# A decoder trunk on one core: the first FFN product by Strassen's seven products of halves, in a fixed order of slots, and the FFN in two parts

## The chip, the core and the metric

The kernel runs on one core of a Trainium2 chip. A core has TensorE (PE in the profile; PEld is its loading of weights), VectorE (DVE), ScalarE (ACT), GpSimd (POOL), and SyncE (SP), whose queue issues most DMA transfers. Each engine works through its own list of instructions in order; semaphores hold an instruction until what it needs is there. PE multiplies a stationary 128x128 tile of weights with a moving tile of up to 512 columns and adds into a bank of PSUM (128 partitions x 512 fp32; there are eight). The metric is the time of one execution on the device in microseconds.

## What is computed

Two decoder layers on one sequence of 512 tokens with 1024 channels. Each has a mixer (layer 0: gated short convolution and pooling; layer 1: attention and a convolution module) and a feed-forward part (FFN), each followed by a residual and a LayerNorm:

```python
D_FF = int(math.ceil((8 * D_MODEL / 3) / 256) * 256)      # 2816
ALPHA = (2.0 * DEPTH) ** 0.25
...
def swiglu(x, w_in, w_out):
    h = x @ w_in
    return (jax.nn.silu(h[..., :D_FF]) * h[..., D_FF:]) @ w_out
...
        x = layer_norm(ALPHA * x + mix, ln_mix_g[layer], ln_mix_b[layer])
        x = layer_norm(ALPHA * x + swiglu(x, ffn_w_in[layer], ffn_w_out[layer]),
                       ln_ffn_g[layer], ln_ffn_b[layer])
```

All is fp32 in and out. The change concerns `swiglu` alone.

## The kernel before

**Exact products.** Each fp32 operand is split into a high half (a copy rounded to fp32r, on ACT: `split`, L84) and a low half (the operand less its high half, on DVE or POOL, L85). A product of two operands is three matmuls: high x high, high x low, low x high (`mm3`, L88 to L90). In the up projection the weights are stationary and the input, kept transposed and split in `xh` and `xl` (128 partitions x 8 x 512), moves.

**The FFN** (`ffn`, L293). It runs over 22 slices n of 128 hidden columns. For each, `load_cols` brings two weight tiles (128x1024, gate and up, 512 KB each) into one of three `raw` buffers and splits them into two of the eight `wt` buffers; `project` then does 2 x 8 x 3 = 48 matmuls of 512 columns into two PSUM banks (slices 0 and 1 in two halves of 256 columns, `SPLIT`). The word pair in this text means such a slice with its gate and up columns. Then silu on ACT (L316), the product on DVE (L318) and a split into `hh` and `hl`, which are kept for all 22 slices. At slice 6 (`XN`) `late_affine` applies the preceding LayerNorm's gain and offset to the residual `xs` on DVE (L202).

**The output projection** (`OutProj`). `first` goes through 11 steps of two slices for the left 512 output columns, with four banks for the four token tiles; `second` does the right 512 columns, the last 5 steps with resident weights token by token, so that `residual` and `norm` of one token tile lie beside the matmuls of the next. `residual` multiplies by ALPHA, adds and takes statistics.

**The order.** A scheduler sets the order of instructions on each engine from priorities, in the attention part PE's list is written out by hand (`tc.manual_schedule`). Buffers of a pool are given out in turn: a tile of a tag with n buffers waits until the tile n places before it is no longer used.

Of the kernel before, what the change touches and what calls it, by code (L numbers as in the profile page):

```python
# [17 lines left out]
P = 128  # L18
S = 512
# [20 lines left out]
SPLIT = [(0, 256), (256, 512)]  # L40
FIRST = 2
DFIRST = 2
DG = 1
XA = 2
XN = 6
XG = (3, 8)
# [12 lines left out]
def trunk(ctx, tc, x, ev_w_in, ev_conv_w, ev_pool_w, ev_pool_scale, ev_w_out, od_w_in,  # L59
# [108 lines left out]

    def load_gb(gb, g, b):
        nc.sync.dma_start(gb[:, 0, :], g.partition_broadcast(P))  # L170
        nc.sync.dma_start(gb[:, 1, :], b.partition_broadcast(P))
        return gb
# [18 lines left out]

    def late_affine(g, b, eng):

        gb = [wtp.tile([P, D], F32, tag="wt", name="gb") for _ in range(2)]
        for dst, v in zip(gb, (g, b)):
            nc.sync.dma_start(dst, v.partition_broadcast(P))
        with tc.high_priority(offset=-CP):
            for t in range(NT):
                for c in range(2):
                    cs = slice(c * 512, (c + 1) * 512)  # L200
                    for v, op in zip(gb, (ALU.mult, ALU.add)):
                        eng.tensor_tensor(xs[t][:, cs], xs[t][:, cs], v[:, cs], op=op)  # L202

    def norm(t, st, gb, ln):
# [11 lines left out]
        for a, b in PIECES:  # L216
            xc, g, b_ = xs[t][:, a:b], gb[:, 0, a:b], gb[:, 1, a:b]
# [12 lines left out]
    class OutProj:  # L230

        def __init__(self, w, order, lhs, resident, resident_pool=lambda kp: None, eng=None):
            self.w, self.order, self.lhs, self.resident = w, order, lhs, resident
            self.resident_pool, self.eng = resident_pool, eng
# [27 lines left out]
        def second(self, gb, ln):  # L264
            KP, order = len(self.order), self.order
            for t in range(NT):
                residual(t, slice(0, 512), self.accs[t][0][0], self.sts[t][:, 0, :])
                self.accs[t] = None
# [4 lines left out]
            for i in range(streamed):  # L273
                ws = self.load(order[i], 512)
                for t in range(NT):
                    self.step(t, i, ws)
            ws = [self.load(kp, 512, self.resident_pool(kp)) for kp in order[streamed:]]
            for t in range(NT):
                for part in range(len(self.accs[t])):
                    acc, cols = self.accs[t][part]  # L280
                    for i in range(streamed, KP):
                        self.step(t, i, ws[i - streamed], part)
                    residual(t, slice(512 + cols.start, 512 + cols.stop), acc, self.sts[t][:, 1 + part, :])
                norm(t, self.sts[t][:, :1 + len(self.accs[t]), :], gb, ln)
# [6 lines left out]


    def ffn(l):  # L293
        w_in, w_out = ffn_w_in[l], ffn_w_out[l]
        with tc.tile_pool(name=f"ffn{l}", bufs=1) as hp:
            pairs = []
            gb = hp.tile([P, 2, D], F32, tag="gb", name="gb") if l else None
            for n in range(NF):
                if n == XN:
                    late_affine(ln_mix_g[l], ln_mix_b[l], nc.vector)  # L300
                if n == 4 and l:
                    load_gb(gb, ln_ffn_g[l], ln_ffn_b[l])
                if n < FIRST and n % FIRST == 0:
# [7 lines left out]
                if n % 2 == 0:  # L311
                    tag = "hA" if n < 10 else "hB"
                    pairs.append([hp.tile([P, 2, S], F32R, tag=tag, name=nm, bufs=10 if n < 10 else 12)
                                  for nm in ("hh", "hl")])
                sg = wk.tile([P, S], F32, tag="sg", name="sg")
# [3 lines left out]
                split(pairs[-1][0][:, n % 2, :], pairs[-1][1][:, n % 2, :], h)  # L319
            out_proj(gb, 1 + 2 * l, w_out, list(range(NF // 2)), lambda k: [y[:, k % 2, :] for y in pairs[k // 2]],  # L320
                     5, lambda kp: [dict(pool_=hp, tag="hA", bufs=10)] * 2)

# [540 lines left out]
```

## Time and profile before

| | |
|---|---|
| runs | 1101.07 us median of 3 (1101.02 to 1101.72) |
| profiled execution | 1100.73 us, its span 1099.0 us |
| granted TensorE clock | 0.994 |
| busy: PE, PEld, DVE, ACT, POOL | 1077.5, 909.8, 529.7, 395.4, 179.9 us |
| FFN of layer 0 | about 165 to 524 us; of layer 1, about 742 us to the end |

In the profile a line like L85 is a line of the kernel before; a helper's line stands for all that call it. Rows of groups show the line, engine, operation, output and input by the program's names, and the shapes; then busy time, mean duration in ns, and the idle time before them with what ended it. In a timeline the columns are start and duration in us. The rows of windows give the busy time of each engine (with its count of instructions), the granted clock, the share of the DMA engines and GB/s.

### The profile page before, as it was taken

Reading aid. Unit: us, or ns where it says so; the run is one execution under the profiler, and the core shown is the slowest. Engines: PE = TensorE matmul, PEld = TensorE weight load, DVE = VectorE, ACT = ScalarE, POOL = GpSimd, SP = SyncE. Lnnn points to the kernel's source line nnn. Section 1 sums busy time; section 2 is a strip of 40 time slices with the busy share of each in tenths; the row PEclk is TensorE's granted clock in tenths of the full one; section 3 lists DMA queues with packets and bytes.
Section 4 is the critical chain, followed back from the end, with each engine's and each line's share of the span. In section 5 each row is a group of like instructions: output and inputs, shape, how many; then the busy total and the mean of one; then the engine's idle time right before and its main releaser. Section 6 shows DMA issues by size and latency. Waiting matters only on the chain.

```text
span 1099.0 us, 13519 instructions
## 1 busy us (share of the span) xinstructions
PE 1077.5 (98%) x5371; PEld 909.8 (83%) x5371; DVE 529.7 (48%) x821; ACT 395.4 (36%) x613; POOL 179.9 (16%) x163
## 2 busy tenths in 40 slices
PE   7999999999999999999999999999999999999997
PEld 7888898888888888888978777898888888888886
DVE  4845464643333332426489978464643333332426
ACT  4333243222223221223476889443222222221210
POOL 2000300000000000012499972700000000000003
PEclk9999999999999999999999999999999999999999
DMA  6423503343333222350333331413343333322312
GB/s 205 120 92 115 153 1 113 98 134 96 96 96 96 96 96 96 115 154 21 78 83 92 98 99 57 134 58 113 99 134 96 96 96 96 96 96 96 115 39 77
DMA packets 150332, 108.30 MB, mean 99 GB/s; under 512 B 5256, under 2 KB 131768, under 8 KB 150270
## 3 DMA queue, kind: packets, MB, share of 16 engines
q1 hardware_dynamic: 149648, 107.11, 32.4%
q8 instruction: 42, 0.69, 0.3%
q10 hardware_dynamic: 622, 0.34, 0.1%
q14 instruction: 20, 0.16, 0.0%
HBM read 103.17 MB, written 2.10 MB: 96 GB/s over the span
## 4 chain that ended last, share of the span: by engine, by line
PE 93%; DVE 2%; ACT 2%; DMA 1%; POOL 1%; issue 1%; SPq 0%; POOLq 0%
PE fl L88 12%; PE fl L90 12%; PE fl L89 12%; PE sc L88 9%; PE sc L90 9%; PE sc L89 9%; PE py L88 4%; PE py L89 4%; PE py L90 4%; PE cv L89 4%; PE cv L90 4%; PE cv L88 4%; PE tp L132 1%; DMA x<-in_x 1%; DVE cv L466 1%
## 5 line engine op out<-in xcount | busy, mean ns | idle before, releaser
L84 ACT ACTIVATE w<-raw 128x1024 fp32r<-128x1024 f32 x176 | 186.0, 1060 | 538.6 <-PE sc L89 176.7
L85 DVE TENSOR_TENSOR w<-raw,w 128x1024 fp32r<-128x1024 f32 x148 | 180.7, 1224 | 288.1 <-ACT w L84 287.9
L85 POOL TENSOR_TENSOR w<-raw,w 128x1024 fp32r<-128x1024 f32 x28 | 67.4, 2416 | 429.1 <-ACT w L84 415.5
L89 PE MATMUL sc<-xl,w 128*128 128x512 f32 (+1 forms) x360 | 129.9, 361 | 0.0
L90 PE MATMUL sc<-xh,w 128*128 128x512 f32 (+1 forms) x360 | 129.6, 361 | 0.0
L88 PE MATMUL sc<-xh,w 128*128 128x512 f32 (+1 forms) x360 | 129.4, 362 | 0.0
L88 PE MATMUL fl<-xh,w 128*128 128x512 f32 (+1 forms) x352 | 128.6, 366 | 0.0
L89 PE MATMUL fl<-xl,w 128*128 128x512 f32 (+1 forms) x352 | 128.4, 365 | 0.0
L90 PE MATMUL fl<-xh,w 128*128 128x512 f32 (+1 forms) x352 | 128.3, 365 | 0.0
L166 POOL TENSOR_TENSOR rs<-rs,neghalf 128x1 f32<-128x1 f32 x20 | 14.4, 720 | 413.6 <-DVE rs L165 413.6
L90 PEld LDWEIGHTS sc<-xh,w 128*128 128x128 f32 x360 | 68.0, 189 | 10.3
L89 PEld LDWEIGHTS sc<-xl,w 128*128 128x128 f32 x360 | 68.0, 189 | 10.3
L88 PEld LDWEIGHTS sc<-xh,w 128*128 128x128 f32 x360 | 67.6, 189 | 10.3
L89 PEld LDWEIGHTS fl<-xl,w 128*128 128x128 f32 x352 | 66.5, 189 | 10.5
L88 PEld LDWEIGHTS fl<-xh,w 128*128 128x128 f32 x352 | 66.4, 189 | 10.6
L90 PEld LDWEIGHTS fl<-xh,w 128*128 128x128 f32 x352 | 66.3, 189 | 10.6
L89 PE MATMUL fl<-w,hh 128*128 128x512 f32 (+1 forms) x176 | 66.3, 377 | 0.0
L88 PE MATMUL fl<-w,hh 128*128 128x512 f32 (+1 forms) x176 | 66.1, 376 | 0.0
L90 PE MATMUL fl<-w,hl 128*128 128x512 f32 (+1 forms) x176 | 66.1, 376 | 0.0
L466 DVE SCALAR_TENSOR_TENSOR cv<-hp,par,cv 128x512 f32<-128x512 f32 x84 | 63.1, 751 | 5.8 <-ACT cv L454 4.5
L89 PE MATMUL py<-xl,w 128*128 128x512 f32 (+1 forms) x160 | 58.9, 368 | 0.0
L88 PE MATMUL py<-xh,w 128*128 128x512 f32 (+1 forms) x160 | 58.9, 368 | 0.0
(364 smaller groups left out, 2050.4 us busy)
## 6 DMA issues: line engine op xcount, KB each, us to landing
raw<-in_ffn_w_in SPq DMA_DIRECT2D x88, 512.0 KB
raw<-in_ffn_w_out SPq DMA_DIRECT2D x44, 512.0 KB
raw<-in_od_w_in SPq DMA_DIRECT2D x20, 512.0 KB
raw<-in_ev_w_in SPq DMA_DIRECT2D x16, 512.0 KB
raw<-in_ev_w_out SPq DMA_DIRECT2D x8, 512.0 KB
raw<-in_od_w_out SPq DMA_DIRECT2D x8, 512.0 KB
x<-in_x SPq DMA_DIRECT2D x4, 512.0 KB
qk<-qk SPq DMA_DIRECT2D x16, 128.0 KB
```

What stands on the lines that cost most here:

```text
L84: nc.scalar.activation(hi, src, AF.Copy)
L85: (eng or nc.vector).tensor_tensor(lo, src, f32(hi), op=ALU.subtract)
L88: nc.tensor.matmul(acc, lh, rh, start=start, stop=False)
L89: nc.tensor.matmul(acc, lh, rl, start=False, stop=False)
L90: nc.tensor.matmul(acc, ll, rh, start=False, stop=stop)
L132: nc.tensor.transpose(tp[:, j * P:(j + 1) * P], xs[t][:, k * P:(k + 1) * P], ident)
L166: nc.gpsimd.tensor_tensor(rs[:, 1:2], rs[:, 0:1], neghalf, op=ALU.pow)
L466: V.scalar_tensor_tensor(acc if i == KCONV - 1 else part, hp[:, i:i + S], tap(i), part, op0=ALU.mult, op1=ALU.add)
```

## The change

Slices 0 to 3 (`PLAIN`) are projected as before. The other 18 are taken two at a time, nine groups a layer. A group's 256 gate and 256 up columns and the 1024 input channels make a 2x2 matrix of blocks of weights (512 channels x 256 columns, the tiles `q11`, `q21`, `q22`, `q12`, of 128x4x256, 512 KB each), and the input is a 2x2 matrix of blocks too (512 channels x 256 tokens). Instead of eight products of blocks the group has seven (Strassen's, in Winograd's form):

- The input's combinations are made once per layer (`moving`, 10 sums on DVE and four splits); one of them overwrites a block of `xh` and `xl`, after the plain slices have used it.
- Of the weights, four sums S1 to S4 per group (DVE, L369), and seven operands are split: high halves on ACT (`hi`, L376), low halves on DVE (`lo`, L380), in three pairs of buffers `sw`.
- Each product is 2 x 4 x 3 = 24 matmuls of 256 columns (L388). Products add up in PSUM banks x (`fl`), y (`sc`) and z (`py` or `cv`); partial sums are kept by three copies on ACT (c1, u2, u3: L396) and joined by DVE (`gate`, L403; u3, L438 and L486). `silu` and `times` act on halves of 256 tokens, `final` splits the result into `hh` and `hl`.

PE's slots in a group are P1, P4 of the last group, P2, P3 of the last group, P6, P5, P7. The order on PE, ACT and DVE is the one of the code (`manual_schedule`); after the last group of a part `closing` does its P4 and P3. The FFN has two parts: slices 0 to 11 with the output projection of these (`OutProj.first` in the fixed order, six steps, the affine steps of `xs` between them; `second` for the right columns, added to `xs` with ALPHA and without statistics), then slices 12 to 21 and their output projection, added with factor 1.

DVE's list in layer 0 before, in the steady part (L85 makes a weight's or a result's low half, L318 the gated result; the numbers are buffers):

```order
L318 TENSOR_TENSOR h_2022<-cv_1957,sg_2020 128x512
L85 TENSOR_TENSOR w_2105<-raw_2102,w_2104 128x1024
L85 TENSOR_TENSOR hl_2019<-h_2022,hh_2018 128x512
L85 TENSOR_TENSOR w_2169<-raw_2166,w_2168 128x1024
L318 TENSOR_TENSOR h_2090<-fl_2027,sg_2088 128x512
L85 TENSOR_TENSOR w_2175<-raw_2172,w_2174 128x1024
```

DVE's list now at the turn from one group to the next (`sw` halves from L380; `sum` S4 and the next S1; L410 `times`; L417 the final low half):

```order
L380 TENSOR_TENSOR sw_2042<-sum_2015,sw_2041 128x1024
L369 TENSOR_TENSOR sum_2047<-sum_1947,q12_1746 128x1024
L369 TENSOR_TENSOR sum_2080<-q21_1917,q22_1919 128x1024
L380 TENSOR_TENSOR sw_2078<-q11_1915,sw_2077 128x1024
L410 SCALAR_TENSOR_TENSOR g_1784<-u3_1906,g_1784 128x2x256
L380 TENSOR_TENSOR sw_2110<-q22_1744,sw_2109 128x1024
L417 TENSOR_TENSOR hl_1694<-g_1784,hh_1693 128x1024
L438 TENSOR_TENSOR u3_2139<-u3_2139,sc_2049 128x512
L380 TENSOR_TENSOR sw_2142<-q12_1921,sw_2141 128x1024
L369 TENSOR_TENSOR sum_2180<-sum_2080,q11_1915 128x1024
```

A slice had four operations; now the next group's P1, the last group's result, P4 and P2 stand in one sequence, in which each waits for those ahead of it. ACT at the same place, before and now (L84, L86 and L376 high halves; L316 and L406 silu; L396 copies; L415 the final high half):

```order
L84 ACTIVATE w_2726<-raw_2724 128x1024
L84 ACTIVATE hh_2570<-h_2642 128x512
L84 ACTIVATE w_2788<-raw_2786 128x1024
L316 ACTIVATE sg_2710<-fl_2646 128x512
L84 ACTIVATE w_2794<-raw_2792 128x1024
L84 ACTIVATE hh_2708<-h_2712 128x512
```

Now ACT makes all of this at the turn of a group:

```order
L376 ACTIVATE sw_2041<-sum_2015 128x1024
L406 ACTIVATE g_2012<-g_2012 128x2x256
L396 ACTIVATE u2_2074<-fl_1881 128x512
L406 ACTIVATE g_1784<-g_1784 128x2x256
L376 ACTIVATE sw_2077<-q11_1915 128x1024
L415 ACTIVATE hh_1693<-g_1784 128x1024
L376 ACTIVATE sw_2109<-q22_1744 128x1024
L396 ACTIVATE u3_2139<-fl_1881 128x512
L376 ACTIVATE sw_2141<-q12_1921 128x1024
```

ACT's copies u2 and u3 and both silu now stand among the high halves that PE needs next. The end of the up projection, ACT, before and now (now: the end of part 1):

```order
L84 ACTIVATE hh_2846<-h_2850 128x512
L84 ACTIVATE w_2992<-raw_2990 128x1024
L316 ACTIVATE sg_2916<-fl_2854 128x512
L84 ACTIVATE w_3022<-raw_3020 128x1024
L84 ACTIVATE hh_2846<-h_2918 128x512
L84 ACTIVATE w_3052<-raw_3050 128x1024
```

ACT now, from the last group of part 1 into the output projection:

```order
L415 ACTIVATE hh_1913<-g_2245 128x1024
L376 ACTIVATE sw_2559<-q22_2152 128x1024
L396 ACTIVATE u3_2564<-fl_2347 128x512
L376 ACTIVATE sw_2566<-sum_2503 128x1024
L406 ACTIVATE g_2468<-g_2468 128x2x256
L415 ACTIVATE hh_2146<-g_2468 128x1024
L86 ACTIVATE w_2635<-raw_2633 128x1024
L86 ACTIVATE w_2641<-raw_2639 128x1024
```

Before, the output projection's weights follow each other from the last slices on; now the first of them (`w_2635`) stands behind the copy u3, P3's operand, the last silu and the final high half. Last, the opening on DVE, before (slices 2 and 3) and now (`T` and `xl_79` are the input's combinations, `h_1656` the last plain slice):

```order
L85 TENSOR_TENSOR w_1665<-raw_1662,w_1664 128x1024
L318 TENSOR_TENSOR h_1588<-cv_1523,sg_1586 128x512
L85 TENSOR_TENSOR w_1671<-raw_1668,w_1670 128x1024
L85 TENSOR_TENSOR hl_1585<-h_1588,hh_1584 128x512
L85 TENSOR_TENSOR w_1735<-raw_1732,w_1734 128x1024
L318 TENSOR_TENSOR h_1656<-fl_1593,sg_1654 128x512
```

DVE now, from the first group's sum S1 (`sum_1706`) to the low half of its first P6:

```order
L369 TENSOR_TENSOR sum_1706<-q21_1697,q22_1699 128x1024
L380 TENSOR_TENSOR sw_1704<-q11_1695,sw_1703 128x1024
L380 TENSOR_TENSOR sw_1735<-q12_1701,sw_1734 128x1024
L87 TENSOR_TENSOR xl_79<-comb_1667,xh_78 128x4x256
L87 TENSOR_TENSOR T_1685<-comb_1683,T_1684 128x1024
L521 TENSOR_TENSOR h_1656<-fl_1593,sg_1654 128x512
L369 TENSOR_TENSOR sum_1748<-sum_1706,q11_1695 128x1024
L87 TENSOR_TENSOR hl_1585<-h_1656,hh_1584 128x512
L380 TENSOR_TENSOR sw_1778<-sum_1748,sw_1777 128x1024
```

The first group's operands P1 and P2 stand ahead of the rest of the input's combinations, and the sum S2 (`sum_1748`), from which P6 is made, behind them and behind the last plain slice's result.

The diff, cut to its core:

```diff
+PLAIN = 4
+PART = 12
...
-    def residual(t, cols, acc, st):
+    def residual(t, cols, acc, st, alpha=ALPHA):
         xc = xs[t][:, cols]
-        nc.vector.scalar_tensor_tensor(xc, xc, ALPHA, acc, op0=ALU.mult, op1=ALU.add)
-        nc.vector.bn_stats(st, xc)
+        if alpha == 1.0:
+            nc.vector.tensor_tensor(xc, xc, acc, op=ALU.add)
+        else:
+            nc.vector.scalar_tensor_tensor(xc, xc, alpha, acc, op0=ALU.mult, op1=ALU.add)
+        if st is not None:
+            nc.vector.bn_stats(st, xc)
...
+    def affine_steps(g, b, eng):
...
+        return [lambda t=t, cs=slice(c * 512, (c + 1) * 512), v=v, op=op:
+                eng.tensor_tensor(xs[t][:, cs], xs[t][:, cs], v[:, cs], op=op)
+                for t in range(NT) for c in range(2) for v, op in zip(gb, (ALU.mult, ALU.add))]
...
+    class Strassen:
...
+        def moving(self):
...
+            t3, T3 = new(), tile2()
+            less(V, t3, B[1, 1], B[0, 1])
+            t1 = new()
+            less(V, t1, B[0, 0], B[0, 1])
+            t2, T2 = new(), tile2()
+            minus(t2, t1, B[1, 1])
+            split(*T2, t2)
+            split(*T3, t3)
+            split(*B[0, 1], t1)
+            t4, T4 = new(), tile2()
+            minus(t4, t2, B[1, 0])
+            split(*T4, t4)
+            self.B = dict(P1=B[0, 0], P2=B[1, 0], P3=B[1, 1], P4=T4, P5=B[0, 1], P6=T2, P7=T3)
...
+        LEFT = dict(P1="11", P2="12", P3="S4", P4="22", P5="S1", P6="S2", P7="S3")
+        def hi(self, g, name):
+            g["A"][name] = [self.hp.tile([P, 4 * 256], F32R, tag="sw", name="sw", bufs=6).rearrange(
+                "p (k c) -> p k c", c=256) for _ in range(2)]
+            nc.scalar.activation(g["A"][name][0], g["raw"][self.LEFT[name]], AF.Copy)
+        def lo(self, g, name):
+            hi, lo = g["A"][name]
+            nc.vector.tensor_tensor(lo, g["raw"][self.LEFT[name]], f32(hi), op=ALU.subtract)
+        def product(self, g, name, bank, start=False, stop=False):
+            (ah, al), (bh, bl) = g["A"][name], self.B[name]
+            for i in range(2):
+                acc, cols = bank[:, i * 256:(i + 1) * 256], slice(i * P, (i + 1) * P)
+                for k in range(4):
+                    for m, (l, r) in enumerate(((ah, bh), (ah, bl), (al, bh))):
+                        nc.tensor.matmul(acc, l[:, k, cols], r[:, k, :], start=start and i == k == m == 0,
+                                         stop=stop and i == 1 and k == 3 and m == 2, skip_group_check=True)
...
+        def copy(self, g, name, tag):
+            g[name] = wk.tile([P, 512], F32, tag=tag, name=name)
+            nc.scalar.activation(g[name], g["x"], AF.Copy)
...
+        def times(self, g, j):
+            h = self.halves(g["h"], j)
+            nc.vector.scalar_tensor_tensor(h, self.whole(g["u3"] if j else g["x"]), -1.0, h, op0=ALU.mult, op1=ALU.mult)
...
+        def opening(self, g):
+            self.hi(g, "P1")
+            self.add(g, "S1", "21", "22")
+            self.lo(g, "P1")
+
+        def group(self, g, last, load_next):
...
+            g["x"] = psum("fl")
+            self.product(g, "P1", g["x"], start=True)
+            if_last(lambda: self.copy(last, "u3", "h"))
+            self.hi(g, "P2")
+            if_last(lambda: V.tensor_tensor(last["u3"], last["u3"], last["y"], op=ALU.add))
+            self.lo(g, "P2")
+            following = load_next()
+            if_last(lambda: self.product(last, "P4", last["x"], stop=True))
+            self.add(g, "S2", "S1", "11")
+            if_last(lambda: self.hi(last, "P3"))
+            if_last(lambda: self.lo(last, "P3"))
+            self.copy(g, "c1", "h")
+            g["z"] = psum(next(self.z))
+            self.product(g, "P2", g["z"], start=True, stop=True)
+            if_last(lambda: self.times(last, 0))
+            self.hi(g, "P6")
+            self.lo(g, "P6")
+            if_last(lambda: self.product(last, "P3", last["y"], stop=True))
+            self.hi(g, "P5")
+            self.gate(g, 0)
+            self.lo(g, "P5")
+            self.add(g, "S3", "11", "21")
+            self.product(g, "P6", g["x"])
+            self.hi(g, "P7")
+            if_last(lambda: self.gate(last, 1))
+            self.lo(g, "P7")
+            self.silu(g, 0)
+            self.add(g, "S4", "S2", "12")
+            g["y"] = psum("sc")
+            self.product(g, "P5", g["y"], start=True)
+            self.copy(g, "u2", "sg")
+            if_last(lambda: self.silu(last, 1))
+            if following:
+                self.opening(following)
+            if_last(lambda: self.times(last, 1))
+            self.product(g, "P7", g["x"])
+            if_last(lambda: self.final(last, "hi"))
+            self.hi(g, "P4")
+            self.lo(g, "P4")
+            if_last(lambda: self.final(last, "lo"))
+            return following
+        def closing(self, last):
...
+            self.copy(last, "u3", "h")
+            self.hi(last, "P3")
+            V.tensor_tensor(last["u3"], last["u3"], last["y"], op=ALU.add)
+            self.lo(last, "P3")
+            self.product(last, "P4", last["x"], stop=True)
+            self.times(last, 0)
+            self.product(last, "P3", last["y"], stop=True)
+            self.gate(last, 1)
+            self.silu(last, 1)
+            self.times(last, 1)
+            self.final(last, "hi")
+            self.final(last, "lo")
...
+            with tc.manual_schedule(engines=FIXED):
+                groups(range(PLAIN, PART, 2))
+                steps = affine_steps(ln_mix_g[l], ln_mix_b[l], nc.vector)
+                o = OutProj(w_out, list(range(PART // 2)), lhs, 0)
+                o.ws = {i: o.load(i, 0) for i in range(2)}
+                for i in range(PART // 2):
+                    if i + 2 < PART // 2:
+                        o.ws[i + 2] = o.load(i + 2, 0)
+                    for step in steps[3 * i:3 * i + 3]:
+                        step()
+                    o.first(i)
+            o.second(None, None)
+            with tc.manual_schedule(engines=FIXED):
+                groups(range(PART, NF, 2))
...
+            out_proj(gb, 1 + 2 * l, w_out, list(range(PART // 2, NF // 2)), lhs, 4,
+                     lambda kp: [next(spare), next(spare)], alpha=1.0)
```

More of the change, by code (lines that the diff above doesn't have):

```diff
@@ L196, in late_affine @@
             nc.sync.dma_start(dst, v.partition_broadcast(P))
-        with tc.high_priority(offset=-CP):
[L198 to L202, printed above, removed]
+        return [lambda t=t, cs=slice(c * 512, (c + 1) * 512), v=v, op=op:
+                eng.tensor_tensor(xs[t][:, cs], xs[t][:, cs], v[:, cs], op=op)
+                for t in range(NT) for c in range(2) for v, op in zip(gb, (ALU.mult, ALU.add))]
+    def late_affine(g, b, eng):
+        steps = affine_steps(g, b, eng)
+        with tc.high_priority(offset=-CP):
+            for step in steps:
+                step()
     def norm(t, st, gb, ln):
@@ L266, in second @@
             for t in range(NT):
-                residual(t, slice(0, 512), self.accs[t][0][0], self.sts[t][:, 0, :])
+                residual(t, slice(0, 512), self.accs[t][0][0], None if ln is None else self.sts[t][:, 0, :],
+                         self.alpha)
                 self.accs[t] = None
@@ L276, in second @@
                     self.step(t, i, ws)
+            if ln is None:
+                for t in range(NT):
+                    residual(t, slice(512, D), self.accs[t][0][0], None, self.alpha)
+                return
             ws = [self.load(kp, 512, self.resident_pool(kp)) for kp in order[streamed:]]
@@ L282, in second @@
                         self.step(t, i, ws[i - streamed], part)
-                    residual(t, slice(512 + cols.start, 512 + cols.stop), acc, self.sts[t][:, 1 + part, :])
+                    residual(t, slice(512 + cols.start, 512 + cols.stop), acc, self.sts[t][:, 1 + part, :],
+                             self.alpha)
                 norm(t, self.sts[t][:, :1 + len(self.accs[t]), :], gb, ln)
@@ L296, in ffn, with new_pair @@
             pairs = []
[L297 to L302, printed above, removed]
+            def new_pair():
+                pairs.append([hp.tile([P, 2, S], F32R, tag="h", name=nm, bufs=PART) for nm in ("hh", "hl")])
+                return pairs[-1]
+            lhs = lambda k: [y[:, k % 2, :] for y in pairs[k // 2]]
+            for n in range(PLAIN):
                 if n < FIRST and n % FIRST == 0:
@@ L311, in ffn @@
                 if n % 2 == 0:
-                    tag = "hA" if n < 10 else "hB"
-                    pairs.append([hp.tile([P, 2, S], F32R, tag=tag, name=nm, bufs=10 if n < 10 else 12)
-                                  for nm in ("hh", "hl")])
+                    new_pair()
                 sg = wk.tile([P, S], F32, tag="sg", name="sg")
@@ L319, in ffn, with groups @@
                 split(pairs[-1][0][:, n % 2, :], pairs[-1][1][:, n % 2, :], h)
-            out_proj(gb, 1 + 2 * l, w_out, list(range(NF // 2)), lambda k: [y[:, k % 2, :] for y in pairs[k // 2]],
-                     5, lambda kp: [dict(pool_=hp, tag="hA", bufs=10)] * 2)
+            st = Strassen(hp)
+            st.moving()
+            hp.tile([P, SHIFT], F32, tag="shift", name="shift")
+            def groups(ns):
+                ns, last = list(ns), None
+                load = lambda: st.load(w_in, ns.pop(0), new_pair()) if ns else None
+                g = load()
+                st.opening(g)
+                while g:
+                    g, last = st.group(g, last, load), g
+                st.closing(last)
+            FIXED = {mybir.EngineType.PE, mybir.EngineType.Activation, mybir.EngineType.DVE}
+            with tc.manual_schedule(engines=FIXED):
[7 more added lines that the diff above has]
+                    for step in steps[3 * i:3 * i + 3]:
+                        step()
+                    o.first(i)
+            o.second(None, None)
+            with tc.manual_schedule(engines=FIXED):
+                groups(range(PART, NF, 2))
+            gb = None
+            if l:
+                g_, b_ = (hp.tile([P, 4 * 256], F32, tag="sw", name="gb", bufs=6) for _ in range(2))
+                nc.sync.dma_start(g_, ln_ffn_g[l].partition_broadcast(P))
+                nc.sync.dma_start(b_, ln_ffn_b[l].partition_broadcast(P))
+                gb = g_, b_
+            spare = iter([dict(pool_=hp, tag="T", bufs=6)] * 6 + [dict(pool_=hp, tag="sw", bufs=6)] * 2)
+            out_proj(gb, 1 + 2 * l, w_out, list(range(PART // 2, NF // 2)), lhs, 4,
+                     lambda kp: [next(spare), next(spare)], alpha=1.0)
     par = const.tile([P, 4, 38], F32, tag="par", name="par")
```

66 lines of the change are left out of this document (57 added, 9 removed).

## The prediction

> **What bounds the kernel now.** I read the page's engine rows first, then the busy time by stage, then single instructions.
>
> ```profile
> span 1099.0 us, 13519 instructions
> PE 1077.5 (98%) x5371; PEld 909.8 (83%) x5371; DVE 529.7 (48%) x821; ACT 395.4 (36%) x613; POOL 179.9 (16%) x163
> L84 ACT ACTIVATE w<-raw 128x1024 fp32r<-128x1024 f32 x176 | 186.0, 1060 | 538.6 <-PE sc L89 176.7
> L85 DVE TENSOR_TENSOR w<-raw,w 128x1024 fp32r<-128x1024 f32 x148 | 180.7, 1224 | 288.1 <-ACT w L84 287.9
> ```
>
> TensorE (PE) is busy 98% of the span; VectorE (DVE) and ScalarE (ACT) mostly wait. By stage (columns: PE, weight loads, DVE, ACT, POOL, granted clock, DMA share, GB/s), the first two rows are the FFN of layer 0, its 256-column start and its steady pairs:
>
> ```profile
> 165.00:176.00 11.00, 11.00 (x94) 11.00 (x93) 4.97 (x5) 5.95 (x7) 0.00 (x0) 1.00 0.29 86
> 176.00:405.00 229.00, 229.00 (x1013) 189.69 (x1013) 87.80 (x100) 66.02 (x84) 0.00 (x0) 1.00 0.34 103
> 405.00:501.00 96.00, 96.00 (x425) 79.42 (x425) 31.37 (x35) 21.74 (x21) 5.33 (x3) 1.00 0.39 119
> ```
>
> PE has no gap in the FFN, while DVE works 88 of 229 us. So two things decide here: how many matmuls there are and how fast they follow each other. Matmul records overlap, so the pace is the distance of starts. At 512 columns, then at 256:
>
> ```profile
> 301.46 0.39 PE L88 MATMUL sc<-xh,w 128*128 128x512 f32 x1
> 306.67 0.39 PE L90 MATMUL sc<-xh,w 128*128 128x512 f32 x1
> 306.90 0.39 PE L88 MATMUL py<-xh,w 128*128 128x512 f32 x1
> ...
> 165.27 0.28 PE L89 MATMUL fl<-xl,w 128*128 128x256 f32 x1
> 176.19 0.28 PE L90 MATMUL sc<-xh,w 128*128 128x256 f32 x1
> ```
>
> The first and third rows are 24 matmuls apart: 5.44 us, 0.2267 each. The last two are 91 apart: 10.92 us, 0.1200 each.
>
> **The saving.** A group of two pairs is 96 matmuls of 512 columns now, 96 x 0.2267 = 21.76 us. As seven products it is 7 x 24 = 168 of 256 columns, 168 x 0.1200 = 20.16 us, 2.88 a slot. Half-width matmuls eat most of Strassen's eighth: 1.60 us a group, and 9 groups in 2 layers make 28.8 us. Break-even is 21.76 / 168 = 0.1295 us a matmul. The second FFN product has its 528 matmuls a layer in either kernel.
>
> A rule speaks against this. The Trainium skill, "TensorE: Matmul & The Clock Gate", section Back-to-back issue gap, gives sustained pairs of weight load and matmul as about 81 ns at 128 columns and 131 ns at 512. Halfway by columns, 256 would cost an estimated 98 ns, 0.75 of the wide one; the group would be 16.4 against 12.6 and the change a loss of some 30% of the stage. This trace has 0.53 (0.1200 to 0.2267), so I go by the rows.
>
> **What the other engines now do per group.** Durations, from the same steady stretch:
>
> ```profile
> 301.48 1.06 ACT L84 ACTIVATE w<-raw 128x1024 fp32r<-128x1024 f32 x1 [3.83 <-PE sc L89]
> 302.44 0.58 ACT L316 ACTIVATE sg<-sc 128x512 f32<-128x512 f32 x1
> 302.57 1.23 DVE L85 TENSOR_TENSOR w<-raw,w 128x1024 fp32r<-128x1024 f32 x1 [3.61 <-ACT w L84]
> 307.17 0.69 DVE L318 TENSOR_TENSOR h<-sc,sg 128x512 f32<-128x512 f32 x1 [3.37 <-PE sc L90]
> 308.01 1.22 DVE L85 TENSOR_TENSOR w<-raw,w 128x1024 fp32r<-128x1024 f32 x1 [0.15 <-ACT w L84]
> 309.15 0.68 DVE L85 TENSOR_TENSOR hl<-h,hh 128x512 fp32r<-128x512 f32 x1
> ```
>
> A 1024-wide DVE operation takes 1.22, and the next starts 1.14 after it (308.01, 309.15); a 512-wide one takes 0.69, 0.61 in a row by the same overlap. ACT: 1.06 and 0.58, in a row 0.96 and 0.5. ACT hands to DVE in 0.03 (302.54 to 302.57). From the slot's end on PE (306.90, when the next product starts) to DVE's start at 307.17 are 0.27.
>
> DVE per group: seven low halves, four operand sums and the final low half are 12 x 1.14 = 13.7; one u3 sum, two gates and two multiplications 5 x 0.61 = 3.05. Together 16.75 of 20.16 us (83%), against 87.80 / 229 = 38% before. ACT: eight x 0.96 and five x 0.5, 10.2 us. DMA brings the same 2 MB a group, so its share goes from 0.34 to about 0.37.
>
> Does it fit in this order? I laid the fixed order's rows end to end, t = 0 at the start of P1. The longest chain begins when P6 ends, t = 14.40: +0.27 the u2 copy, 0.5, silu 0.5, high of the next P1 1.06, +0.03 its low 1.14, the multiplication 0.69, +0.03 the final high 0.96, high of P4 1.06, +0.03 low of P4 1.22: 21.9. P4 is due at 23.04 (its slot starts 2.88 into the next group), the low half 0.24 later, at its third matmul. Going on: final low half, u3 sum, low of P2, ready at 24.8, due at 25.92. The other products are earlier. So a steady group has about 1.1 to 1.3 us in hand and costs PE nothing; DVE's 3.4 us of waits are the cover.
>
> A second rule bears on this: the Trainium skill, "VectorE: DVE Perf Modes", section Terms, says that a flush after every DVE operation keeps the next from issuing until the pipe is empty. By it DVE's group would be 12 x 1.22 + 5 x 0.69 = 18.1 us, an estimate, and by my laying-out about 0.4 us a group would be lost, 7 in all. Row 309.15 starts 0.08 before row 308.01 ends, so the rule isn't taken.
>
> **Where PE will wait, per layer.**
> (a) Opening. P6 of the first group needs sum S2. After the low half of P1 (about t = 0.5; I take 0.3 of wait there, bounds 0 and 2, since DVE's preparing operations run until just then) DVE has low P2, the split of xl, low T4: 3 x 1.14; then `h` of the last plain pair 0.61; S2 1.22; then ACT's high 1.06: t = 6.9 against 5.76 + 0.3, 0.8 late. The low half comes 1.25 after the high, needed 0.24 after it: 1.0 more. Sum 2.1.
> (b) Closing of part 1: P4 follows P7 at once and waits for ACT's u3 copy of the same bank: 0.27 + 0.58 and hand-overs, 1.0.
> (c) Closing, after P3: the output product's first weights stand behind the group's end on ACT. 0.27, gate 0.69, silu 0.58, multiplication 0.69, final high 0.96, high of w 1.06, hand-overs 0.15: 4.4 until the first matmul. Its second needs w's low half: final low half and that one on DVE, ready at 5.9. PE loses about 5.7.
> (d) Part 2: low of P6 in its first group 0.15, next P1 0.13, P4 at its closing 0.6 (two output matmuls stand ahead): 0.9. Its output weights are split ahead of the end, so (c) isn't repeated.
> Sum 9.7 a layer, 19.4 in all; bounds 12 (a and d hidden) and 28.
>
> (e) A long idle slows PE's clock afterwards. In the attention stage PE had nothing to start between the first two rows below:
>
> ```profile
> 601.58 0.28 PE L90 MATMUL fl<-w,xl 128*128 128x256 f32 x1
> 604.94 0.50 PE L658 MATMUL sc<-qk 68*128 68x512 f32 x1 [3.08 <-DMA qk<-aug]
> 606.35 0.63 PE L88 MATMUL fl<-xh,wqh 128*128 128x512 f32 x1
> 606.77 0.63 PE L89 MATMUL fl<-xl,wqh 128*128 128x512 f32 x1
> 604.00:608.00 4.00, 3.06 (x9) 2.18 (x10) 3.93 (x9) 3.35 (x8) 4.00 (x5) 0.69 0.05 11
> 608.00:612.00 4.00, 4.00 (x21) 3.42 (x21) 3.11 (x8) 2.66 (x8) 3.18 (x3) 0.88 0.87 257
> ```
>
> Then 512-column matmuls are 0.42 apart, not 0.2267; the clock's means 0.69 and 0.88 are 4 x 0.31 / 0.5 + 4 x 0.12 / 0.5 = 3.4 us at half speed, a loss of up to 1.7. The wait in (c) is longer than 3.36, so I expect the same in each layer, less what falls into the wait itself: 1.2 each (bounds 0 and 1.7), 2.4.
>
> Costed at nothing: the affine steps, now three after each output weight's split (1.14 + 3 x 0.61 = 3.0 of DVE in 5.44 of PE); the first part's residual without statistics; in SP's queue the two `gb` loads ahead of twelve output weights, whose issue waits for buffers long free; layer 1's `gb` at the end, with 4 x 5.44 us of output steps ahead of it. If that cover is gone, each late load costs its landing, a few us.
>
> **Sum.** -28.8 + 19.4 + 2.4 = -7.0 us, against the profiled execution's 1100.73 us (span 1099.0 and 1.7 around it): 1093.7. The median of the runs, 1101.07, lies 0.3 higher: 1094.0.
>
> **Rivals.**
> (1) Slower: DVE doesn't hold the slots. The place is the chain of P4 and P2, with 1.1 to 1.3 us in hand of 10.4: when its links are 12% longer than these rows (four loads at once, handovers that cost 0.1), each group waits. A loss of 28.8 - 21.8 = 7.0 spread over 18 groups, 0.39 us each, cancels the gain; at 0.8 it is 1094 + 14.4 = 1108. For it: DVE goes from 38% to 83% in an order that nothing can overtake. Against: 1224 ns is the mean of 148 operations, with little spread in the trace. The VectorE rule above would put the time here, at about 0.4 a group. Chance 0.28; with under 0.6 a group it ends about unchanged (0.12), else slower (0.16).
> (2) 256-column matmuls don't hold 0.1200 over 20 us. Weight loads are busy 11.00 of 11.00 us there, nothing in hand. At 0.1295 the saving is gone: 1094 + 28.8 = 1123. Against: the stretch of 91 has no slower step. The TensorE rule above would end far on this side. Chance 0.04.
> (3) Better: opening and clock cost nothing, as DVE is ahead and the slow stretch falls into the wait: -28.8 + 2 x (5.7 + 1.0) = -15.4, 1086. Chance 0.13.
>
> **Chances.** The forecast has 0.55 (1090 to 1099). A measurement of this kernel tells about 0.2%, 2.2 us, from no change: faster 0.55 + 0.13 = 0.68, same 0.12, slower 0.20. The range 1087 to 1107 leaves out half of (3), the upper part of (1) and (2).
>
> **What will show it.** PE matmuls from 5371 records to about 5371 + 18 x 72 - 36 = 6631 (six of the last layer's output steps no longer go by halves for the last token tile); in the steady groups PE without gaps at 0.120, 2.88 us a product; a stretch of about 5.7 us between P3 and the first output matmul, twice, with a lower clock behind it; DVE near 83% there. Wrong if PE waits in every group, for `sw` halves from DVE or ACT, or if the gaps at the closings are under 3 us.

## The result, and the profile after

The changed kernel takes 1082.28 us (median of 4, 1081.43 to 1084.19) against 1101.05 us (4 runs, 1100.87 to 1101.72): ratio 0.983, 95% interval 0.9818 to 0.9843. I had forecast 1094.0, range 1087 to 1107: the side is right, the gain is 18.8 us instead of 7, and the time lies below the range. The profiled execution took 1084.19 us.

The page of the changed kernel (engine busy times, share of the span, instructions):

```profile
span 1082.5 us, 16331 instructions
PE 1046.3 (97%) x6631; PEld 938.1 (87%) x6631; DVE 744.3 (69%) x1027; ACT 482.6 (45%) x711; POOL 179.5 (17%) x163
```

There are 1260 matmul records more, as worked out, and 31 us less of busy PE. In what follows a step is the time from the start of one matmul to the start of the next. Timeline of PE in a group of part 1 of layer 0 and in one of part 2 (start, duration; a row x24 is a whole product):

```profile
226.58 2.99 PE L388 MATMUL fl<-T,sw 128*128 128x256 f32 x24
229.41 0.28 PE L388 MATMUL sc<-xh,sw 128*128 128x256 f32 x1
...
380.12 2.88 PE L388 MATMUL fl<-T,sw 128*128 128x256 f32 x24
382.84 0.28 PE L388 MATMUL sc<-xh,sw 128*128 128x256 f32 x1
```

A product's slot is 2.83 us in the one and 2.72 in the other: 117.8 and 113.3 ns a matmul. I had forecast 2.88, from 120.0, so these matmuls are cheaper than I took them to be. And 113.3 is half of a 512-column matmul's 226.7. Between two waits of PE all products keep one of these two steps. The plain halves at the opening still go at 120.0. By stage (columns as in the prediction: PE, weight loads, DVE, ACT, POOL, granted clock, DMA share, GB/s): the opening, a steady group of each part, the closing of part 1, and the stretch behind it.

```profile
198.57:212.03 13.46, 11.73 (x97) 11.13 (x96) 11.73 (x13) 5.80 (x9) 0.00 (x0) 1.00 0.34 101
220.93:240.71 19.78, 19.78 (x170) 19.78 (x169) 15.65 (x16) 10.76 (x13) 0.00 (x0) 1.00 0.35 107
374.68:393.72 19.04, 19.04 (x170) 19.04 (x169) 15.00 (x16) 10.77 (x13) 0.00 (x0) 1.00 0.35 110
278.33:285.41 7.08, 2.88 (x26) 2.68 (x24) 3.04 (x4) 2.68 (x4) 0.00 (x0) 1.00 0.22 74
285.71:292.54 6.83, 5.93 (x14) 4.46 (x14) 5.26 (x6) 1.55 (x2) 0.00 (x0) 0.50 0.59 179
```

Groups take 19.78 and 19.04 us, not 20.16, and PE has no gap in them. At the closing PE is busy 2.88 of 7.08 us, and afterwards runs at half clock for 6.83 us. In PE's timeline:

```profile
280.93 0.28 PE L388 MATMUL sc<-xh,sw 128*128 128x256 f32 x1
285.41 0.55 PE L90 MATMUL fl<-w,hh 128*128 128x512 f32 x1 [4.21 <-ACT w L86]
286.86 0.79 PE L91 MATMUL fl<-w,hh 128*128 128x512 f32 x1 [0.90 <-DVE w L87]
...
291.72 0.63 PE L90 MATMUL sc<-w,hh 128*128 128x512 f32 x1
292.15 0.58 PE L91 MATMUL sc<-w,hh 128*128 128x512 f32 x1
292.57 0.40 PE L92 MATMUL sc<-w,hl 128*128 128x512 f32 x1
```

The last matmul of P3 and the first of the output projection are 4.48 us apart, with the weight's high half on ACT (L86) ending the wait, as in term (c); the low half on DVE ends the next. From 287.45 to 292.57 the matmuls are 0.43 apart. The Trainium skill, "TensorE: Matmul & The Clock Gate", section What's actually happening, says that the activity window behind this is 3413 ns long and runs free: the stretch of 6.83 us is two such windows, and the two rows of before that I had gone by were one.

One line of the change explains the step, and I had neither costed it nor shown it (the diff above leaves it out):

```diff
+SHIFT = 16
...
+            hp.tile([P, SHIFT], F32, tag="shift", name="shift")
```

It puts 64 bytes ahead of the buffers `sw`. In the built program they then begin at byte 195680 of a partition and at 4096-byte steps from there, 96 modulo 256; `xh`, `xl`, `T` and the plain weights all begin at 32 modulo 256. Offset below means this distance of the weights from the moving data.

### The profile page after: what moved, and what is told of

Read it like the earlier page. It is cut to its first block, busy times and chain, and to the rows that moved or that the text cites. A ratio compares the mean times of both kernels' runs of the same rounds, so it can differ in the third digit from the quotient of the medians.

```text
span 1082.5 us, 16331 instructions
## 1 busy us (share of the span) xinstructions
PE 1046.3 (97%) x6631; PEld 938.1 (87%) x6631; DVE 744.3 (69%) x1027; ACT 482.6 (45%) x711; POOL 179.5 (17%) x163
## 4 chain that ended last, share of the span: by engine, by line
PE 81%; DVE 8%; ACT 4%; issue 3%; DMA 2%; POOL 1%; SPq 0%; POOLq 0%; ACTq 0%; DVEq 0%
PE fl L388 14%; PE fl L91 9%; PE fl L92 9%; PE fl L90 9%; PE sc L388 7%; PE sc L91 5%; PE sc L92 5%; PE sc L90 5%; DVE sw L380 3%; PE py L91 2%; PE py L90 2%; PE py L92 2%; DVE sum L369 2%; PE cv L388 2%; PE cv L92 2%
## 5 line engine op out<-in xcount | busy, mean ns | idle before, releaser
L86 ACT ACTIVATE w<-raw 128x1024 fp32r<-128x1024 f32 x104 | 109.0, 1057 | 207.8 <-PE sc L91 77.9
L388 PE MATMUL fl<-T,sw 128*128 128x256 f32 x1296 | 160.5, 279 | 4.3 <-DVE sw L380 1.5
L388 PEld LDWEIGHTS fl<-T,sw 128*128 128x128 f32 x1296 | 153.9, 188 | 6.9 <-ACT u L396 2.5
L87 DVE TENSOR_TENSOR w<-raw,w 128x1024 fp32r<-128x1024 f32 x76 | 92.4, 1223 | 92.1 <-ACT w L86 91.7
L376 ACT ACTIVATE sw<-sum 128x1024 fp32r<-128x1024 f32 x72 | 76.0, 1060 | 104.6 <-DVE sum L369 73.5
L380 DVE TENSOR_TENSOR sw<-sum,sw 128x1024 fp32r<-128x1024 f32 x72 | 88.0, 1222 | 26.2 <-ACT sw L376 26.2
L388 PE MATMUL sc<-xh,sw 128*128 128x256 f32 x576 | 105.5, 278 | 0.0
L388 PEld LDWEIGHTS sc<-xh,sw 128*128 128x128 f32 x576 | 89.9, 188 | 0.1
L380 DVE TENSOR_TENSOR sw<-q,sw 128x1024 fp32r<-128x1024 f32 x54 | 65.4, 1221 | 29.2 <-ACT sw L376 29.1
L168 POOL TENSOR_TENSOR rs<-rs,neghalf 128x1 f32<-128x1 f32 x20 | 13.6, 681 | 402.2 <-DVE rs L167 396.2
L388 PE MATMUL sc<-xl,sw 128*128 128x256 f32 x288 | 80.1, 278 | 0.0
L376 ACT ACTIVATE sw<-q 128x1024 fp32r<-128x1024 f32 x54 | 56.3, 1050 | 45.3 <-DMA q<-in_ffn_w_in 45.3
L369 DVE TENSOR_TENSOR sum<-q,q 128x1024 f32<-128x1024 f32 x36 | 43.9, 1219 | 25.7 <-DMA q<-in_ffn_w_in 25.7
L388 PE MATMUL fl<-xh,sw 128*128 128x256 f32 x288 | 53.8, 281 | 1.6 <-DVE sw L380 1.6
L90 PE MATMUL sc<-xh,w 128*128 128x256 f32 (+1 forms) x168 | 54.9, 331 | 0.0
L92 PE MATMUL sc<-xh,w 128*128 128x256 f32 (+1 forms) x168 | 54.8, 328 | 0.0
```

What stands on the lines that cost most here:

```text
L86: nc.scalar.activation(hi, src, AF.Copy)
L87: (eng or nc.vector).tensor_tensor(lo, src, f32(hi), op=ALU.subtract)
L90: nc.tensor.matmul(acc, lh, rh, start=start, stop=False)
L92: nc.tensor.matmul(acc, ll, rh, start=False, stop=stop)
L168: nc.gpsimd.tensor_tensor(rs[:, 1:2], rs[:, 0:1], neghalf, op=ALU.pow)
L369: nc.vector.tensor_tensor(raw[name], raw[a], raw[b], op=ALU.add)
```

## Experiments

### Where the pace comes from

The expectations of the first three runs here don't know of that line. The changed kernel again:

> The changed kernel once more, nothing edited, as the base for the others and to see whether the pace of its half-width matmuls repeats. In its first profile products ran at 113.3 ns a matmul or at 117.8, and changed only at a wait of PE. Theory (the pace is a state that a wait sets by chance): time 1081 to 1084.5 us; in part 1 of layer 0 again a step of 113.3 or 117.8 and nothing between, but not at all places the same as before (the last group of part 2 was 117.8 in layer 0 and 113.3 in layer 1, for the same instructions). Rival (the pace belongs to the place in the code): every product at the pace that it had in the first profile.

Measured: 1085.35 us (4 runs, 1083.35 to 1085.72). The group that began at 374.68 went at the fast step; now, at the same place:

```profile
380.33 2.99 PE L388 MATMUL fl<-T,sw 128*128 128x256 f32 x24
383.16 0.28 PE L388 MATMUL sc<-xh,sw 128*128 128x256 f32 x1
```

2.83 us. All 669 matmuls of part 2 behind the wait at 368.5 are at 117.8 here. Those of part 1 of layer 1 behind the wait for the second group's P1, one stretch of 501 at 117.8 in the first profile, are at 113.3 with two short waits between. So the place in the code doesn't decide between these two; each stretch keeps the step that it took up at its last wait. Over all products the mean is 116.4 ns here and 115.3 in the first profile, 18 x 168 x 1.1 ns = 3.3 us. The two profiled spans themselves lie only 1.2 us apart (1083.7 and 1082.5): at 117.8 PE has fewer short waits inside the groups, and the stretches outside the products differ too. So the step explains a part of the 3.1 us between the two medians, and how large a part isn't shown.

The kernel before, all pairs in halves (`ALL` replaced by `SPLIT` in `ffn`):

> The kernel before with all its pairs in halves of 256 columns (20 pairs a layer more than before), no Strassen: twice as many matmuls, same arithmetic. It prices a 256-column matmul outside the products. A pair is 48 x 0.2267 = 10.88 us; as 96 matmuls of 0.1200 it is 11.52, of 0.1178 11.31, of 0.1133 10.88. Theory (0.1200, as I read it in the opening stretch, is what such a matmul costs in the plain projection, and the products are different): 1101.05 + 40 x 0.64 = 1126.6 us. Rival 1 (0.1200 belonged to the opening stretch; in a long stretch without waits it goes at 0.1178): 1118. Rival 2 (half a wide one everywhere but at the opening): 1101 to 1103.

Measured: 1127.7 us (1125.73 to 1128.26), ratio 1.0235 (1.0218 to 1.0252). It is the theory's number: in the plain projection the price that I had read, 120.0, holds over whole layers. Then the products differ in something. A probe with five kinds of plain halves (plain, wide, short, wide and short, other) between pairs of 512:

```diff
-                    project(accs, [load_cols(w_in, n * P), load_cols(w_in, DFF + n * P)], ALL)
+                    probe(n, accs, w_in, hp)
```

> The kernel before with eight to nine of its pairs a layer in halves of 256 columns, in four kinds, between pairs of 512: plain (as at the opening), wide (weights laid out as in the products, 4 x 256 with gate beside up), short (12 matmuls to a half of a bank, then 12 to the other, as in the products), wide and short, and other (weights in buffers of another pool). It is to tell what makes 256-column matmuls go at 120.0 ns in the projection and at 117.8 or 113.3 in the products. Theory 1 (the weights' layout): wide and wide short at 117.8 or 113.3, the rest at 120.0. Theory 2 (the order by halves of a bank): short and wide short below 120.0. Theory 3 (where the weights' buffers lie): other below 120.0, the rest at 120.0. Theory 4 (none of it, but the restart after a wait for an operand): all at 120.0. Time 1101 + 18 x 0.64 = 1112.6 us at 120.0 throughout.

Measured: 1111.2 us (one run). Each kind goes at 120.0 in both layers (medians of 96 steps). Layout, order within a bank and pool are out as causes by themselves; the other pool's buffers begin at 32 modulo 256 too, so the probe has no offset anywhere. Next, the offset alone:

```diff
-            hp.tile([P, SHIFT], F32, tag="shift", name="shift")
```

> The changed kernel without the 64-byte tile that it puts ahead of the buffers sw (the products' weights). With it these buffers begin 64 bytes further within a partition than all other operands (96 bytes modulo 128, where the input's tiles and the plain projection's weights stand at 32). Theory (the offset between weights and moving data decides; the line in the change that I didn't cost is what makes 256-column matmuls cheaper than 120.0 ns): every product at 120.0, groups of 20.16 us instead of 19.04 or 19.79; from the two profiles' mix (a mean of 115.3 and 116.3 ns) 18 x 168 matmuls x 4.2 ns = 12.7 us more, less up to 2 us for waits that shrink: 1082.3 + 11.5 = 1094 us. Rival (the products' order on the engines, not the place of the buffers): 113.3 and 117.8 as before, 1081 to 1085.

Measured: 1094.45 us (5 runs, 1093.48 to 1095.65). In its timeline:

```profile
247.21 3.04 PE L388 MATMUL fl<-T,sw 128*128 128x256 f32 x24
250.09 0.28 PE L388 MATMUL sc<-xh,sw 128*128 128x256 f32 x1
```

2.88 us, 120.0 each; the group from 221.29 to 241.45 takes 20.16. The kernel without this line is the one that I had forecast. The reverse, the plain halves with 64 bytes ahead of their weights:

```diff
     rawp = pool("raw", 3)
+    pool("shift").tile([P, 16], F32, tag="shift", name="shift")
     wtp = pool("wt", 8)
```

> The kernel before with all pairs in halves of 256 columns (1127.7 us, 120.0 ns throughout) and a 64-byte tile ahead of its weights' buffers, nothing else. Theory (the offset decides, in any code): the halves at 117.8 or 113.3; since PE doesn't wait there, one pace for nearly a whole layer: 1127.7 - 40 x 96 x 2.2 ns = 1119 us at 117.8, 1102 at 113.3. Rival (the products' order decides): 1127 us, 120.0 throughout.

Measured: 1100.94 us (1099.88 to 1101.65), ratio to the kernel before 0.9996 (0.9986 to 1.0005). PE's timeline, 24 matmuls apart, without the offset and then with it:

```profile
300.00 0.28 PE L90 MATMUL fl<-xh,w 128*128 128x256 f32 x1
...
302.88 0.28 PE L90 MATMUL fl<-xh,w 128*128 128x256 f32 x1
```

```profile
300.06 0.28 PE L90 MATMUL sc<-xl,w 128*128 128x256 f32 x1
...
302.78 0.28 PE L90 MATMUL sc<-xl,w 128*128 128x256 f32 x1
```

2.88 and 2.72 us. Sixty-four bytes are worth 26.8 us in this kernel (1127.7 to 1100.94), and with them the time is that of the kernel before, with half-width matmuls in place of the wide ones. So the step needs neither the products' order nor Strassen.

The same run shows that the distance counts, and not the place of the weights alone. All buffers behind the 64 bytes move with them, so in the output projection weights and moving data both begin at 96 modulo 256. Its halves for the last token tile, 9 matmuls apart:

```profile
1045.80 0.28 PE L91 MATMUL fl<-w,hl 128*128 128x256 f32 x1
...
1046.88 0.28 PE L91 MATMUL sc<-w,hl 128*128 128x256 f32 x1
```

1.08 / 9 = 120.0 ns, as without the 64 bytes. Its 512-column matmuls keep 227 ns in the mean, while the mixers' of 512 columns, whose weights moved and whose input did not, go at 233. Two other offsets, on the best kernel (below): `SHIFT = 8` (32 bytes) and `SHIFT = 32` (128 bytes).

> The best kernel so far (1060.8 us) with an offset of 32 bytes instead of 64. If any offset that isn't a multiple of 128 helps, its products go at 113.3 or 117.8 as before; if only 64 does, at 120.0 (about 1074 us).

> The best kernel so far (1060.8 us) with an offset of 128 bytes instead of 64. If the offset counts modulo 128, its products go at 120.0 as without one, 1060.8 + 18 x 168 x 4.3 ns = 1074 us; if it counts modulo more, they stay at 113.3 or 117.8.

Measured: 1072.4 and 1074.8 us (one run each), against 1060.8 with 64 bytes. PE's timeline at 32 bytes, then at 128:

```profile
245.92 3.00 PE L388 MATMUL fl<-T,sw 128*128 128x256 f32 x24
248.76 0.28 PE L388 MATMUL sc<-xh,sw 128*128 128x256 f32 x1
```

```profile
245.78 3.01 PE L388 MATMUL fl<-T,sw 128*128 128x256 f32 x24
248.63 0.28 PE L388 MATMUL sc<-xh,sw 128*128 128x256 f32 x1
```

2.84 and 2.85 us, 118.3 and 118.7 ns, with steps that change from matmul to matmul (115 to 123). Both expectations fall: 32 bytes is neither as good as 64 nor as bad as none, and 128 isn't quite the same as none, so the offset doesn't count modulo 128. Why the offset acts, and which of two steps a restart takes, stays open.

### The waits that I had forecast

Term (c) and the clock, by splitting the first output weights early:

```diff
             self.lo(last, "P3")
+            if early:
+                early()          # o.ws.update({i: o.load(i, 0) for i in range(2)})
             self.product(last, "P4", last["x"], stop=True)
```

> The changed kernel with the first two output weights of part 1 loaded and split before P4 of the closing, ahead of the last gate, silu, product and final halves. Theory (term c and the clock behind it are the order's price): PE no longer stops after P3, and no slow stretch follows. From P3's end (281.05) to 292.57 in layer 0 the changed kernel started 16 output matmuls, 16 x 0.2267 = 3.63 of 11.52 us, so 7.9 are to be had; in layer 1 from 849.39 to 859.20 12 of them, 2.72 of 9.81, 7.1: 1082.3 - 15.0 = 1067.3 us, granted clock 1.00 in that stretch. Rival 1 (the clock falls whatever the order, the idle only coincides): 1082.3 - 2 x 5.4 = 1071.5, with a stretch of clock 0.5 left. Rival 2 (PE then waits for PSUM banks of the last group, which the late gate frees): a wait of 1 to 3 us in the first output step, 1070 to 1074.

Measured: 1069.46 us (1068.65 to 1070.2), ratio 0.971; 15.9 less than the changed kernel's 1085.35, where 15.0 was expected. PE goes on without a gap, at full clock (its timeline, then the windows):

```profile
279.74 0.28 PE L388 MATMUL sc<-xh,sw 128*128 128x256 f32 x1
279.86 0.40 PE L90 MATMUL fl<-w,hh 128*128 128x512 f32 x1
```

```profile
279.74:300.00 20.26, 20.26 (x92) 16.81 (x91) 14.73 (x20) 5.82 (x6) 0.00 (x0) 1.00 0.43 142
...
764.00:767.20 3.20, 1.71 (x12) 1.42 (x12) 2.67 (x4) 1.72 (x2) 0.00 (x0) 1.00 0.00 0
767.20:770.70 3.50, 3.50 (x19) 3.50 (x19) 2.29 (x3) 1.69 (x3) 0.00 (x0) 0.51 0.10 27
```

Neither rival appears: no slow stretch behind P3, no wait for a bank. But the last two rows, in the opening of layer 1, show a slow stretch at another place: two waits of 0.7 and 0.8 us close together, PE busy 1.71 of 3.20 us, and the clock halves. The changed kernel has like waits (0.5 to 0.8) in both of its openings and kept its clock there. That it depends on how the waits fall into the free-running window (the Trainium skill, "TensorE: Matmul & The Clock Gate", section What's actually happening) would fit, but one profile shows it once, so it isn't shown.

Rival (1) of the prediction, tested by one more operation in the tight chain:

```diff
             self.lo(g, "P4")
+            self.lo(g, "P4")
```

> The changed kernel with the low half of every P4 made twice on DVE (the second writes the same again): 1.14 us more in the chain that the prediction found tightest. In the trace the low half of P4 ended 1.0 us before its use where the matmuls go at 117.8 ns and 0.0 before it where they go at 113.3. Theory (the chain has just that in hand): PE waits 0.15 to 0.3 us for P4 and about as much for P2 in a group of part 1, about 1.1 in one of part 2; groups of about 20.2 us against 19.8 and 19.3, some 1082.3 + 2 x (4 x 0.4 + 5 x 0.9) = 1094 us. Rival (there is more in hand than the laying-out says, since DVE stood idle 2 us before that operation): 1082 to 1085.

Measured: 1098.97 us (10 runs, 1097.97 to 1100.19), 13.6 more than the changed kernel's 1085.35; 12 were expected. In its list of waits (us in all, times, longest), and in DVE's timeline in a group of part 1:

```profile
PE fl L388 <- DVE sw L380: 13.1, 17, 1.3
```

```profile
257.24 2.49 DVE L380 TENSOR_TENSOR sw<-q,sw 128x1024 fp32r<-128x1024 f32 x2 [2.08 <-ACT sw L376]
```

The idle time of 2.08 us ahead of that operation is no reserve, since ACT's high half ends it: 20.5 us more of DVE work cost 13.6 us. So the chain is real. In the changed kernel, DVE's low half of P4 in part 1 (117.8) and part 2 (113.3), each with the start of P4 on PE behind it:

```profile
255.65 1.23 DVE L380 TENSOR_TENSOR sw<-q,sw 128x1024 fp32r<-128x1024 f32 x1 [2.07 <-ACT sw L376]
257.67 0.75 PE L388 MATMUL fl<-T,sw 128*128 128x256 f32 x5
...
409.02 1.23 DVE L380 TENSOR_TENSOR sw<-q,sw 128x1024 fp32r<-128x1024 f32 x1 [2.08 <-ACT sw L376]
410.04 0.65 PE L388 MATMUL fl<-T,sw 128*128 128x256 f32 x3
```

The third matmul of P4 is the first to need this low half, 0.24 after the product's start: 257.91 - 256.88 = 1.0 us in hand, and 410.28 - 410.25 = 0.0. The faster step uses up what the laying-out had found, 1.1 to 1.3.

### Better versions

The high half of P4 ahead of the final high half on ACT:

```diff
-            if_last(lambda: self.final(last, "hi"))
             self.hi(g, "P4")
             self.lo(g, "P4")
+            if_last(lambda: self.final(last, "hi"))
```

> The changed kernel with the high half of P4 put ahead of the last group's final high half on ACT (and so the low half of P4 ahead of DVE's 2 us of idle time). Theory (the chain that is tight at 113.3 ns runs through that wait): the low half of P4 ends about 2 us before its use, the short waits of PE in steady groups (0.03 to 0.18 us beyond a matmul's own step, for P4 and P2) are gone, worth 0.1 to 0.3 us a group where the pace is 113.3, in all 1 to 3 us at most; and since nothing interrupts the products then, each stretch keeps one pace from its last wait in the opening on to the closing. Which of the two it is decides more: groups of 19.04 or of 19.79 us. So 1079 to 1085 us, with no wait inside steady groups. Rival (the short waits go to another product, P2 or P6, since DVE's total is the limit): the same time, waits of the same size elsewhere.

Measured: 1080.56 us (1078.6 to 1082.95), within what the step's chance allows, so the time says nothing; the trace does: from the wait at the second group's P1 on, 501 to 669 matmuls a part without one interruption, in three of the four parts at 113.3. All together, with S4 written over S2 behind the next P1:

```diff
-            self.add(g, "S4", "S2", "12")        # ahead of P5
...
+            g["raw"]["S4"] = g["raw"]["S2"]      # behind the next P1, ahead of hi(g, "P4")
+            nc.vector.tensor_tensor(g["raw"]["S4"], g["raw"]["S2"], g["raw"]["12"], op=ALU.add)
```

> The changed kernel with the output weights split ahead of the closing (as in the earlier run, 1069.5 us), the swap on ACT, and sum S4 written over S2 after the next group's P1 instead of ahead of it, so that the next P1, in the first group of each part late by 0.1 to 0.5 us, comes earlier by 1.14. Theory (what waits are left stand at these places): waits for P1 of the second group and inside steady groups gone, 0.5 to 0.9 us a layer less than the hoisted kernel, 1066 to 1069 us with the same spread from the pace. Rival (DVE's sum of work sets it and S4 comes late for P3 instead): waits of 0.5 us or more at P3, 1070 to 1080.

Measured: 1060.77 us (4 runs, 1059.15 to 1063.84), ratio 0.9635 (0.9621 to 0.965), the best of all. It is better than the 1066 to 1069 expected: the profiled spans of the hoisted kernel and of this one are 1067.5 and 1062.1, and the stops beyond 113.3 and 226.7 ns a step in both FFNs sum to 13.4 us in the one and 7.6 in the other. The medians lie 8.7 apart, so some 3 us of it isn't accounted for. The slow stretch at 767 isn't there (1.6), nor are the waits at the closing of part 2 (1.5), which the expectation had left out. A group with its pace at 113.3:

```profile
219.91:238.95 19.04, 19.04 (x171) 19.04 (x169) 16.72 (x18) 11.02 (x13) 0.00 (x0) 1.00 0.36 114
```

PE without a gap and DVE at 88%. Last, the offset for the other weights too:

```diff
+    pool("pad").tile([P, 16], F32, tag="pad", name="pad")
     wtp = pool("wt", 8)
+    pool("pad2").tile([P, 48], F32, tag="pad2", name="pad2")
```

> The best kernel so far (1060.8 us) with its other weights' buffers moved too: 64 bytes ahead of the buffers wt, 192 behind them, so that wt stands 64 bytes off the input's tiles and all later buffers move by 256. Some 900 matmuls of 256 columns outside the products (mixer projections, the opening of each FFN) went at 119.8 ns. Theory (the offset decides, in any code): they go at 117.8 or 113.3, 900 x 2.0 to 6.5 ns = 2 to 6 us less, 1055 to 1059 us; the products as before. Rival (an offset of 320 bytes between the input's tiles and the products' weights is worse than 64, as 32 and 128 were): the products that read the input's own tiles fall to 118 or more, 1060 to 1066 us.

Measured: 1066.34 us (5 runs, 1062.15 to 1069.76), 5.6 slower by the medians, though the ranges overlap by 1.7. The 256-column matmuls outside the products did gain (116.0 ns in the mean of some 630 steps behind 177 us, 119.8 without), and the products kept 113.3 and 117.8 (mean 115.4 in both kernels): neither theory nor rival. The price is paid by the 512-column ones. PE's timeline at the plain pairs with the offset (6 matmuls apart), and in the kernel without it (8 apart):

```profile
189.28 0.39 PE L92 MATMUL fl<-xh,w 128*128 128x512 f32 x1
...
190.68 0.39 PE L92 MATMUL fl<-xh,w 128*128 128x512 f32 x1
```

```profile
188.73 0.39 PE L90 MATMUL fl<-xh,w 128*128 128x512 f32 x1
...
190.54 0.39 PE L92 MATMUL fl<-xh,w 128*128 128x512 f32 x1
```

1.40 / 6 = 233 ns against 1.81 / 8 = 226. Over 2174 steps of 512 columns the mean is 230.7 and was 227.4, 7 us.

## Why the prediction was wrong

The step that failed is the first term, the saving. "168 x 0.1200 = 20.16" took the price of a 256-column matmul from a stretch whose weights stand at no offset to the moving data, and costed at nothing, without naming it, the line that gives the products' weights an offset of 64 bytes. Without that line the step is 120.0 ns, as forecast; with it, 113.3 or 117.8. With the mean of the first profile, 115.3 ns, a group saves 21.76 - 168 x 0.1153 = 2.39 us, and 18 save 43.0 instead of 28.8. The other terms, by the first profile (stops beyond 113.3 and 226.7 ns a step; the clock's share is what is left of the stretch behind P3 without its first two stops):

| term, us | forecast, both layers | measured, layer 0 + layer 1 |
|---|---|---|
| saving | -28.8 | -43.0 |
| (a) opening | 4.2 | 2.6 + 2.4, and 0.5 + 0.5 for P1 of the second group |
| (b) P4 at the closing | 2.0 | 1.0 + 1.0 |
| (c) first output weights | 11.4 | 5.6 + 5.6 |
| (d) part 2 | 1.8 | 2.0 + 2.3 |
| (e) clock | 2.4 | 2.8 + 2.0 |
| not forecast, between the FFNs | 0 | -2.0 |
| sum (of unrounded terms) | -7.0 | -16.8 |

The spans differ by 16.5. The last row but one: from the last transpose ahead of the attention layer to the first one behind it are 194.1 us before and 192.0 after, with or without the offset; I haven't traced its cause. (a) to (c) are right in place and within 0.5 us a layer in size, but for the second group's P1. (d) and (e) are too small: in part 2 P1 of the second group waits 0.5 and the tight chain another 0.1 to 0.3 in two groups, which follows from the step; and the clock lost two windows where I had put one.

That the kernel without the offset gives 1094.45, the number of the forecast, is partly luck: its stops sum to 24.6 instead of 21.8 us, and 2.0 come back between the FFNs.

Rival (1), DVE not holding the slots, didn't come: at 117.8 DVE holds them with 1.0 us in hand, at 113.3 barely, and the doubled operation shows that this chain is the next limit. Rival (2) looked for the pace to be worse over 20 us; it was better, the side that I gave no chance. The argument behind it, "nothing in hand", stood on weight loads busy 11.00 of 11.00 us; they are busy all of the time at 113.3 too, so that share doesn't say what bounds the step. Rival (3) had the right direction by another mechanism: neither the opening nor the clock was free. The estimate of 0.75 of a whole matmul for a half one, worked out from the figures for 128 and 512 columns that the Trainium skill gives ("TensorE: Matmul & The Clock Gate", section Back-to-back issue gap), is not borne out: 0.53 without the offset, 0.50 to 0.52 with it.

## What to carry to other kernels

Read every line of a change that moves a buffer: a tile that nothing uses was worth 9 to 12 of the 18.8 us here (1094.45 without it, 1085.35 and 1082.28 with it). A matmul's price holds for the place of its operands as well as its width, so before a row's step is carried to new buffers, compare their byte offsets. In these runs weights 64 bytes off the moving data were the best of four offsets for 256 columns, and no offset was better than 64 for 512. At the end of a loop in fixed order, split the next stage's first weights ahead of the last group's tail: that was worth 16 us, nearly half of it through the clock and the second stop behind it.

## What the runs showed of the hardware

- 256-column matmuls (fp32r, weights loaded for each): 120.0 ns with weights and moving data at the same place modulo 256 bytes, 118.3 with the weights 32 bytes further, 113.3 or 117.8 with 64, 118.7 with 128. 512-column ones: 226.7 to 227 at none, 233 at 64. Moving both operands by 64 bytes changes neither.
- At 64 bytes the step is one of two and stays until PE's next wait; which one is not set by the code (the same stretch took either in two runs). That this makes the changed kernel's runs spread by 3 us is not shown: without the offset five runs spread by 2.2 (1093.48 to 1095.65).
- The clock halved for 6.83 us around idle times of PE of 4.2 and 0.7 to 0.9 us, and once for 3.4 us behind two of 0.7 and 0.8.
